# Down projection of f tiles 14 to 17 in seven products of quarters, with fewer weight buffers for it

## The chip, the cores and the metric

The kernel runs on one core of a Trainium2 chip. The time is device microseconds of one launch, the median of the runs. A profiled execution gives the trace. TensorE (PE) multiplies matrices, VectorE (DVE), ScalarE (ACT) and GpSimd (POOL) work on elements, SyncE (SP) issues DMAs; ScalarE and GpSimd can issue DMAs too.

## What is computed

A decoder trunk of two layers for 512 prompt tokens and 8 sequences of 8 sampled tokens, 576 columns together, with a model width of 1024, in float32. Layer 0 begins with a convolution and windowed attention (mixer 0), layer 1 with a Mamba-2 mixer (mixer 1); both then have the feed-forward part that the change is about:

```python
def conv_ffn(h, hist, w_gate, w_up, conv_w, conv_b, w_down):
    gate = h @ w_gate
    padded = jnp.concatenate([hist, gate], axis=1)
    gc = causal_dwconv(padded, conv_w, conv_b)
    y = (jax.nn.silu(gc) * (h @ w_up)) @ w_down
    return y, padded[:, -(FFN_CONV_WIDTH - 1):]
```

w_gate and w_up are 1024 x 2816, w_down is 2816 x 1024: 22 tiles (f = 0 to 21) of 128. Conv states, caches and SSM states are further outputs.

## The kernel before

Everything stays on the chip, transposed: x[m] (m = 0 to 7) are tiles of 128 channels x 576 columns. The columns are cut in two halves of 288. Every operand of a product is split into a high part that TensorE's fast float32 form holds, and the rest. A product of tiles is three matmuls (high by high, high by low, low by high), each 128x128 by 128x288, into one bank of PSUM. ScalarE makes the high part (a copy), VectorE the low part (a difference).

**Gate and up.** The class Strassen does two f tiles at a time in seven products of 12 matmuls where a plain form has eight (p1 to p7, in the Winograd form). It needs sums of weight quarters S1 to S4. `load` fetches the raw weights: the two upper quarters into a buffer `wr` of 1024 columns (`self.up`), the lower right quarter into another (`self.low`), and four slots st0 to st3 of 512 columns are first loaded with one quarter each by SyncE and then get others added by GpSimd's DMAs (`accum_op=ADD`). `alpha`, `beta` and `gamma` split the upper quarters, S1 with S2, and S4 with S3; `sums` splits the lower right one (`dh`, `dl`). The raw buffers come from one ring of three, tag `wr`; down weights use the same ring.

**Order.** In `ffn` the list todo holds 19 jobs after the first ones (Gate 4, Up 2, Gate 6, Up 4, ..., Up 20). In each turn the new job's first products alternate with the last products of the job before (`prev.p3`, `prev.p7`, `prev.p4`), and `some(1)` sets one tile of the down projection between them: 12 matmuls (four f tiles), for one output tile m and one half. `PARTS` cuts the down projection by f into (0, 2), (2, 6), (6, 10), (10, 14), (14, 18), (18, 22); here called parts 0 to 5. Part p starts when its last f tile is ready, part 5 is done after the loop by `out_proj`. `down` takes, per output tile, a buffer's half of down weights (`single` splits it to `vh`, `vl`), eight matrix products of quarters per pair of output tiles, one add to x[m] each (`add_x`). In layer 1 the last job's last product ends around 1440 us of the span; behind each layer's loop the rest of the down projection follows.

The order on each engine is fixed when the program is built, by a scheduler that works with costs of its own and with the pools' free buffers; so a change of buffers can move instructions elsewhere too. `keep_in_program_order` pins the first matmul of a product. `S` hands out slots of 576 columns, 48 small ones and EXTRA further.

## Time and profile before

| | us |
|---|---|
| median of 3 runs | 1482.55 (1481.72 to 1483.52) |
| profiled execution | 1483.3 |
| its span | 1481.5 |
| TensorE busy | 1459.2 (99%) |
| VectorE busy | 1119.0 (76%) |
| ScalarE busy | 822.0 (55%) |
| GpSimd busy | 304.1 (21%) |

The granted clock of TensorE is 0.995 over the span. Busy times come from the page. A matmul's length overlaps the next one's, so TensorE's busy time says only that something was always in flight. In the rows, L with a number is the line of the kernel, `<-` stands between outputs and inputs, and what stands in brackets is the idle time before the instruction with the engine and tile that ended it.

### The profile page before, as it was taken

To read this page: it belongs to the slowest core of one execution; us is meant where nothing else is said; L and a number is where in the kernel's file an instruction comes from. 1 tells how busy PE (TensorE), PEld (TensorE's weight loads), DVE (VectorE), ACT (ScalarE), POOL (GpSimd) and SP (SyncE) were. 2 spreads that over 40 slices of the span, in tenths; PEclk is the share of its full clock that TensorE was granted. 3 is DMA by queue.
4 is the path that set the end of the run, shared out by engine and by line. 5 is a ranking of instruction groups with operands and counts; after the bars stand their busy time and mean duration, and the time that the engine had idled before them with its cause. 6 is when DMAs were issued, how large, how long until landed. Compare 5 with 4: busy or idle time off the path is not lost.

```text
span 1481.5 us, 29273 instructions
## 1 busy us (share of the span) xinstructions
PE 1459.2 (99%) x11179; PEld 1389.9 (94%) x11179; DVE 1119.0 (76%) x2121; ACT 822.0 (55%) x1659; POOL 304.1 (21%) x517
## 2 busy tenths in 40 slices
PE   8999999999999999999999999999999999999999
PEld 7967799999999999998988998997999999999998
DVE  7968799876666665878897777776989766666673
ACT  6357467655445543487764665665457554444450
POOL 0026211222222220011203102102022222232300
PEclk9999999999999999999999999999999999999999
DMA  7604553787777772136245245245366787877841
GB/s 228 164 29 118 160 133 100 195 212 197 184 200 197 191 191 69 58 121 199 72 154 178 86 124 165 86 146 166 105 172 176 193 217 184 211 195 179 212 113 65
DMA packets 120779, 227.60 MB, mean 154 GB/s; under 512 B 25518, under 2 KB 32558, under 8 KB 120638
## 3 DMA queue, kind: packets, MB, share of 16 engines
q1 hardware_dynamic: 98750, 185.87, 39.7%
q0 software_dynamic: 21888, 39.86, 16.3%
q8 instruction: 88, 1.44, 0.4%
q14 instruction: 53, 0.43, 0.1%
HBM read 190.54 MB, written 15.21 MB: 139 GB/s over the span
## 4 chain that ended last, share of the span: by engine, by line
PE 86%; DVE 6%; ACT 4%; DMA 2%; issue 1%; SPq 0%; ACTq 0%; POOL 0%; DVEq 0%
PE mm L313 15%; PE mm L317 15%; PE mm L316 15%; PE x L113 5%; PE x L116 5%; PE x L117 5%; PE y L116 3%; PE y L117 3%; PE y L113 3%; PE mm L622 2%; PE mm L618 2%; PE mm L621 2%; PE z L116 1%; PE z L113 1%; PE z L117 1%; DMA acb<-acd 1%
## 5 line engine op out<-in xcount | busy, mean ns | idle before, releaser
L313 PE MATMUL mm<-hh,wh 128*128 128x288 f32 x864 | 261.0, 303 | 6.0 <-ACT wh L284 5.4
L316 PE MATMUL mm<-hl,wh 128*128 128x288 f32 x864 | 258.8, 300 | 0.9 <-DVE hl L801 0.8
L317 PE MATMUL mm<-hh,wl 128*128 128x288 f32 x864 | 257.5, 298 | 0.5 <-DVE wl L285 0.5
L497 DVE TENSOR_TENSOR x<-x,mm 128x288 f32<-128x288 f32 x288 | 128.6, 449 | 77.6 <-PE mm L317 76.3
L313 PEld LDWEIGHTS mm<-hh,wh 128*128 128x128 f32 x864 | 163.6, 190 | 14.3 <-ACT wh L284 5.9
L313 PE MATMUL mm<-yh,vh 128*128 128x288 f32 x576 | 170.0, 295 | 0.0
L316 PE MATMUL mm<-yl,vh 128*128 128x288 f32 x576 | 169.9, 295 | 0.0
L317 PE MATMUL mm<-yh,vl 128*128 128x288 f32 x576 | 169.8, 295 | 0.0
L316 PEld LDWEIGHTS mm<-hl,wh 128*128 128x128 f32 x864 | 163.5, 189 | 4.4 <-issue 1.6
L317 PEld LDWEIGHTS mm<-hh,wl 128*128 128x128 f32 x864 | 163.6, 189 | 3.5 <-issue 1.6
L284 ACT ACTIVATE wh<-wr 128x1024 fp32r<-128x1024 f32 (+1 forms) x97 | 101.6, 1048 | 102.6 <-PE mm L316 79.0
L285 DVE TENSOR_TENSOR wl<-wr,wh 128x1024 fp32r<-128x1024 f32 (+1 forms) x97 | 119.5, 1236 | 36.3 <-ACT wh L284 35.5
L82 ACT ACTIVATE wh<-st 128x512 fp32r<-128x512 f32 x152 | 91.3, 626 | 57.8 <-PE z L116 36.0
L69 POOL DMA_DIRECT2D st<-st x76 | 67.5, 889 | 262.8 <-DMA st<-st 65.5
L313 PE MATMUL mm<-yh,wh 128*128 128x288 f32 x384 | 115.9, 302 | 0.7 <-DVE x L497 0.7
L317 PE MATMUL mm<-yh,wl 128*128 128x288 f32 x384 | 115.0, 300 | 0.0
L316 PE MATMUL mm<-yl,wh 128*128 128x288 f32 x384 | 114.9, 300 | 0.0
L83 DVE TENSOR_TENSOR wl<-st,wh 128x512 fp32r<-128x512 f32 x152 | 101.3, 688 | 15.9 <-ACT wh L82 12.3
L316 PEld LDWEIGHTS mm<-yl,vh 128*128 128x128 f32 x576 | 108.4, 188 | 0.0
L317 PEld LDWEIGHTS mm<-yh,vl 128*128 128x128 f32 x576 | 108.3, 188 | 0.0
L313 PEld LDWEIGHTS mm<-yh,vh 128*128 128x128 f32 x576 | 108.3, 188 | 0.0
L573 DVE SCALAR_TENSOR_TENSOR gconv<-gbuf,par,gconv 128x592 f32<-128x592 f32 x88 | 73.0, 832 | 32.2 <-ACT gconv L571 31.6
(409 smaller groups left out, 4306.4 us busy)
## 6 DMA issues: line engine op xcount, KB each, us to landing
st<-in_w_up SPq DMA_DIRECT2D x80, 256.0 KB, 4.3
wr<-in_w_down SPq DMA_DIRECT2D x80, 256.0 KB, 3.5
wr<-in_w_in_o SPq DMA_DIRECT2D x40, 512.0 KB, 3.6
st<-st POOLq DMA_DIRECT2D x76, 256.0 KB, 4.7
st<-in_w_gate SPq DMA_DIRECT2D x72, 256.0 KB, 4.6
wr<-in_w_gate SPq DMA_DIRECT2D x26, 512.0 KB, 4.3
wr<-in_w_up SPq DMA_DIRECT2D x24, 512.0 KB, 4.1
st<-in_w_up POOLq DMA_DIRECT2D x40, 256.0 KB, 4.7
```

The lines of the kernel that those rows point to most:

```text
L82: nc.scalar.activation(hi, src, AF.Copy)
L83: nc.vector.tensor_tensor(lo, src, hi.bitcast(F32), op=SUB)
L113: m = nc.tensor.matmul(out, hi[:, ws], xh, start=first and k == 0, stop=False, skip_group_check=skip)
L116: nc.tensor.matmul(out, hi[:, ws], xl, start=False, stop=False, skip_group_check=skip)
L117: nc.tensor.matmul(out, lo[:, ws], xh, start=False, stop=k == 3, skip_group_check=skip)
L284: nc.scalar.activation(hi[:, a:b], raw[:, a:b], AF.Copy)
L285: nc.vector.tensor_tensor(lo[:, a:b], raw[:, a:b], hi[:, a:b].bitcast(F32), op=SUB)
L313: first = nc.tensor.matmul(out, hi[:, ws], xh[:, sl], start=i == 0, stop=False)
L316: nc.tensor.matmul(out, hi[:, ws], xl[:, sl], start=False, stop=False)
L317: nc.tensor.matmul(out, lo[:, ws], xh[:, sl], start=False, stop=i == n - 1)
L497: nc.vector.tensor_tensor(self.x[m][:, sl], self.x[m][:, sl], p[:, :HB], op=ADD)
L573: nc.vector.scalar_tensor_tensor(cv[:, :592], g[:, k:592 + k], w(k), cv[:, :592], op0=MUL, op1=ADD)
```

## The change

`SEVEN = (4,)` sends part 4 (f = 14 to 17) through `down7`: the f tiles are cut in a left pair (14, 15) and a right pair (16, 17), the output tiles in pairs m, m + 1, the columns in the two halves, and the same seven products of quarters are formed as for gate and up, six matmuls each: 42 in place of 48 per pair of output tiles. `quarters_of` forms the activation quarters (B11, B21, B22, T1 to T4) once per layer with `combine` and `operand`; the weight sums s1 to s4 are formed on VectorE for each pair of output tiles, and each of three buffers of 512 columns (`single`) and one `dd` is split. A product is added to, or subtracted from, x[m] right after its matmuls (`add`): seven adds per pair in place of four. Partial results of one pair stay in two banks, `dx` and `dy`, which later products add to.

To make room, S3 and S4 are no longer loaded: GpSimd's DMAs add the other quarters to the upper weights where they lie, after `alpha` has split these. So `self.up` is held until `gamma`. The lower right quarter goes to a slot of its own, `a22`. During the job loop two of the three buffers are for upper weights (`ring_up`) and one for down weights (`ring_wr`); behind the loop they are one ring again. The conv state that is read (`fhist`) and the one that is written share one slot, there is one more slot in all, and wide tiles take odd slots.

```diff
+SEVEN = (4,)
...
-        self.up = b.weights_load(up, 1024)
-        s1, s2, s3, s4 = self.s = [b.S(f"st{i}", 512) for i in range(4)]
-        for s, first, more in ((s1, low[:, 512:1024], low[:, 0:512]), (s2, up[:, 0:512], s1), (s4, up[:, 512:1024], s2),
-                               (s3, up[:, 0:512], low[:, 0:512])):
-            self.nc.sync.dma_start(s, first)
+        self.up = b.weights_load(up, 1024, b.ring_up)
+        s1, s2 = [b.S(f"st{i}", 512) for i in range(2)]
+        s3, s4 = self.up[:, 0:512], self.up[:, 512:1024]
+        self.s = s1, s2, s3, s4
+        self.nc.sync.dma_start(s1, low[:, 512:1024])
+        self.nc.sync.dma_start(s2, up[:, 0:512])
+        self.low = b.S("a22", 512)
+        self.nc.sync.dma_start(self.low, low[:, 512:1024])
+        self.alpha()
+        for s, more in ((s1, low[:, 0:512]), (s2, s1), (s3, low[:, 0:512]), (s4, s2)):
             self.nc.gpsimd.dma_start(s, more, accum_op=ADD)
-        self.low = b.weights_load(low[:, 512:1024], 512)
-        self.alpha()
...
-    EXTRA = 14
+    EXTRA = 15
...
+        self.ring_wr = [0, 1, 2]
...
-    def weights_load(self, src, n):
-        raw = self.wp.tile([P, 1024], F32, tag="wr", bufs=3, name="wr")
+    def weights_load(self, src, n, ring=None):
+        ring = ring or self.ring_wr
+        ring.append(ring.pop(0))
+        raw = self.wp.tile([P, 1024], F32, tag=f"wr{ring[-1]}", bufs=1, name="wr")
...
-        hist, so = self.S("fhist", NF * 16), self.S("fso", NF * 16)
+        hist = so = self.S("fhist", NF * 16)
...
+        def down7(p):
...
+            def quarters_of(name):
+                if name == "B22":
+                    t[name] = [operand("yq", v[:, right]) for v in vs]
+                elif name == "T1":
+                    t[name] = [operand("yT", combine(u[:, left], u[:, left], u[:, right], SUB)) for u in us]
...
+            def add(m, half, bank, op):
+                x = self.x[m][:, HALF[half]]
+                nc.vector.tensor_tensor(x, x, bank[:, :HB], op=op)
+
+            load(0)
+            first = self.single(raw[0][:, 0:2 * n])
+
+            def go():
+                for m in range(0, 8, 2):
+                    a11, a12, a21, a22 = [raw[m][:, i * n:i * n + n] for i in range(4)]
+                    w = self.single(raw[m][:, 0:2 * n]) if m else first
+                    s12, s43 = self.S("sd", 512), self.S("sd", 512)
+                    s1, s2, s4, s3 = s12[:, 0:n], s12[:, n:2 * n], s43[:, 0:n], s43[:, n:2 * n]
+                    nc.vector.tensor_tensor(s1, a21, a22, op=ADD)
+                    nc.vector.tensor_tensor(s2, s1, a11, op=ADD)
+                    x, z = self.ps("dx"), self.pm()
+                    product(x[:, :HB], w, 0, t["B11"], True)
+                    add(m, 0, x, ADD)
+                    product(z[:, :HB], w, n, t["B21"], True)
+                    add(m, 0, z, ADD)
+                    w = self.single(s12[:, 0:2 * n])
+                    nc.vector.tensor_tensor(s3, a11, a21, op=ADD)
+                    nc.vector.tensor_tensor(s4, a12, s2, op=ADD)
...
+                    nc.scalar.activation(dh, a22, AF.Copy)
+                    nc.vector.tensor_tensor(dl, a22, dh.bitcast(F32), op=SUB)
+                    load(m + 2)
...
+                    yield
+                    y = self.ps("dy")
+                    product(y[:, :HB], w, 0, t["T1"], True)
+                    add(m + 1, 1, y, SUB)
+                    product(x[:, :HB], w, n, t["T2"], False)
+                    add(m, 1, x, ADD)
+                    w = self.single(s43[:, 0:2 * n])
...
+                    yield
+                    product(y[:, :HB], w, 0, t["B22"], False)
+                    add(m, 1, y, ADD)
+                    product(x[:, :HB], w, n, t["T3"], False)
+                    add(m + 1, 1, x, SUB)
...
+                    yield
+                    product(x[:, :HB], (dh, dl), 0, t["T4"], False)
+                    add(m + 1, 0, x, SUB)
...
+        self.ring_up, self.ring_wr = self.ring_wr[:2], self.ring_wr[2:]
...
-                tiles = down(ready)
+                tiles = (down7 if ready in SEVEN else down)(ready)
...
+        self.ring_wr = self.ring_up + self.ring_wr
```

TensorE issues 48 matmuls fewer, VectorE 108 instructions more, ScalarE 39 more (36 splits and 3 table loads, the latter in mixer 1), SyncE 76 DMAs fewer; GpSimd has as many as before. Lines move: the old L497 (add to x) is L506, L1243 is L1376, L1016 is L1149; L800 is the add of `down7`, L811, L812, L819 and L820 form its weight sums, L825 and L303 are VectorE's halves of its splits, L597 and L595 those of the activation quarters.

Three places show the move. The first is VectorE near the end of mixer 0: `ca` is the convolution's output, `lsum` the sum over channels for the layer norm (whose mean TensorE forms, `pm`). Before:

```order
L1016 TENSOR_SCALAR ca_2043<-mm_1977,par_72 128x512
L1243 TENSOR_TENSOR lsum_2069<-lsum_2069,ca_2043 128x288
L1017 TENSOR_SCALAR ca_2043<-mm_1978,par_72 128x64
L1243 TENSOR_TENSOR lsum_2069<-lsum_2069,ca_2043 128x288
L1246 TENSOR_TENSOR ca_395<-ca_395,pm_2082 128x288
```

Now:

```order
L1149 TENSOR_SCALAR ca_2043<-mm_1977,par_72 128x512
L89 TENSOR_TENSOR dl_3177<-a22_3166,dh_3176 128x512
L1376 TENSOR_TENSOR lsum_2069<-lsum_2069,ca_2043 128x288
L1150 TENSOR_SCALAR ca_2043<-mm_1978,par_72 128x64
L1376 TENSOR_TENSOR lsum_2069<-lsum_2069,ca_2043 128x288
L1379 TENSOR_TENSOR ca_395<-ca_395,pm_2082 128x288
```

The low part of the first job's lower right weights (`a22`, in the old kernel a `wr` buffer, split much later) now stands between a step of `ca` and its sum.

The second is SyncE at the end of layer 1's loop. `st` and `a22` and the `wr` from `in_w_up` belong to jobs, the `wr` from `in_w_down` to the down projection. Before:

```order
L68 DMA st3_17614<-in_w_up 128x512
L68 DMA st2_17613<-in_w_up 128x512
L68 DMA st1_17612<-in_w_up 128x512
L273 DMA wr_17623<-in_w_up 128x512
L273 DMA wr_17717<-in_w_down 128x512 x2
L783 DMA out_ffn_p<-fpo_13433 128x44
L782 DMA out_ffn_s<-fso_13431 128x352
L273 DMA wr_17904<-in_w_down 128x512 x2
L273 DMA wr_18001<-in_w_down 128x512 x2
L273 DMA wr_18066<-in_w_down 128x512 x2
L273 DMA wr_18131<-in_w_down 128x512 x2
L273 DMA wr_18196<-in_w_down 128x512 x2
```

Now:

```order
L282 DMA wr_17568<-in_w_up 128x1024
L71 DMA st1_17571<-in_w_up 128x512
L73 DMA a22_17574<-in_w_up 128x512
L70 DMA st0_17570<-in_w_up 128x512
L916 DMA out_ffn_p<-fpo_13425 128x44
L915 DMA out_ffn_s<-fhist_13423 128x352
L282 DMA wr_17987<-in_w_down 128x512 x2
L282 DMA wr_17641<-in_w_down 128x512 x2
L282 DMA wr_18052<-in_w_down 128x512 x2
L282 DMA wr_17838<-in_w_down 128x512 x2
L282 DMA wr_18182<-in_w_down 128x512 x2
L282 DMA wr_18117<-in_w_down 128x512 x2
```

wr_17987, wr_18052, wr_18182 and wr_18117 are the final projection's chunks; the third and fourth pair's chunks of part 4 (wr_17641, wr_17838) stand among them, since they wait for the one buffer, and wr_18117 waits for wr_17838's.

The third is VectorE at the same place, where the last pairs of part 4 are added up. `mm`, `dx` and `dy` are PSUM banks, x0 to x7 the result, `gsilu` and `yl` activations. Before:

```order
L497 TENSOR_TENSOR x3_80<-x3_80,mm_17773 128x288
L294 TENSOR_TENSOR vl_17842<-wr_17717,vh_17841 128x512
L672 SCALAR_TENSOR_TENSOR gsilu_17162<-x_17418,gsilu_17162 128x288
L336 TENSOR_TENSOR yl_17801<-gsilu_17162,yh_17800 128x576
L285 TENSOR_TENSOR wl_18070<-wr_18066,wh_18069 128x1024
L659 TENSOR_TENSOR st_13894<-st_13894,y_17759 128x288
L661 TENSOR_TENSOR gsilu_17470<-gsilu_17470,st_13894 128x288
L497 TENSOR_TENSOR x4_81<-x4_81,mm_17845 128x288
L336 TENSOR_TENSOR yl_17838<-gsilu_17470,yh_17837 128x576
L657 SCALAR_TENSOR_TENSOR st_13894<-st_13894,x_17639 128x288
```

Now:

```order
L800 TENSOR_TENSOR x4_81<-x4_81,dx_17813 128x288
L303 TENSOR_TENSOR vl_17913<-wr_17838,vh_17912 128x512
L820 TENSOR_TENSOR sd_17917<-wr_17838,sd_17916 128x256
L696 SCALAR_TENSOR_TENSOR gsilu_17552<-x_17594,gsilu_17552 128x288
L800 TENSOR_TENSOR x4_81<-x4_81,dy_17855 128x288
L345 TENSOR_TENSOR yl_17888<-gsilu_17552,yh_17887 128x576
L800 TENSOR_TENSOR x5_82<-x5_82,dx_17813 128x288
L303 TENSOR_TENSOR vl_17937<-sd_17916,vh_17936 128x512
L800 TENSOR_TENSOR x5_82<-x5_82,dx_17813 128x288
L506 TENSOR_TENSOR x0_77<-x0_77,mm_17994 128x288
L294 TENSOR_TENSOR wl_18121<-wr_18117,wh_18120 128x1024
L800 TENSOR_TENSOR x6_83<-x6_83,dx_17920 128x288
```

Where an add to x stood between splits of whole operands, adds of one pair now alternate with splits (L303) and sums (L820) of quarters, and the split of the final projection's third chunk (L294) stands ahead of the fourth pair's first add.

More of the change, by code (lines that the diff above doesn't have):

```diff
@@ L77, in sums @@
         self.d = b.S("dh", 512, F32R), b.S("dl", 512, F32R)
-        self.split(self.low[:, 0:512], *self.d)
+        self.split(self.low, *self.d)
+        b.free(self.low)
     def split(self, src, hi, lo):
@@ L102, in gamma @@
         self.w3 = self.two(self.s[3], self.s[2])
-        self.b.free(self.s[3], self.s[2])
     def product(self, bank, w, col, q, first):
@@ L176, in S @@
     def S(self, name, n=T, dt=F32, rows=P):
-        i = self.idle.pop(0)
+        i = next((i for i in self.idle if n <= T or i % 2), self.idle[0])
+        self.idle.remove(i)
         pool = self.sp if i < self.NSLOT else self.ep
@@ L579, in gate_done, with operand @@
             self.free(g, cv)
-        def up_done(f):
+        def operand(name, src, sign=1.0):
+            q = self.S(name, T, F32R)
+            hi, lo = q[:, 0:HB], q[:, HB:T]
+            nc.scalar.activation(hi, src, AF.Copy, scale=sign)
+            if sign < 0:
+                nc.vector.scalar_tensor_tensor(lo, src, sign, hi.bitcast(F32), op0=MUL, op1=SUB)
+            else:
+                nc.vector.tensor_tensor(lo, src, hi.bitcast(F32), op=SUB)
+            return q
+        def up_done(f):
+            for p in SEVEN:
+                a, b = PARTS[p]
+                if a <= f < b:
+                    y_of[f] = operand("yq", sl_of[f][:, HALF[0]]) if f < (a + b) // 2 else None
+                    return
             y_of[f] = self.pair("y")
@@ L725, in down, with product @@
             return go()
+        def product(out, w, col, xs, first):
+            hi, lo = w
+            for k, q in enumerate(xs):
+                ws = slice(col + k * P, col + k * P + P)
+                m = nc.tensor.matmul(out, hi[:, ws], q[:, 0:HB], start=first and k == 0, stop=False, skip_group_check=not first)
+                if k == 0:
+                    self.tc.keep_in_program_order(m)
+                nc.tensor.matmul(out, hi[:, ws], q[:, HB:T], start=False, stop=False, skip_group_check=not first)
+                nc.tensor.matmul(out, lo[:, ws], q[:, 0:HB], start=False, stop=k == len(xs) - 1, skip_group_check=not first)
@@ L781, in ffn @@
         some(16)
+        self.ring_wr = self.ring_up + self.ring_wr
         nc.sync.dma_start(d["ffn_s"][l], so)
         nc.sync.dma_start(d["ffn_p"][l], po)
-        self.free(so, hist, self.sr, list(self.hq.values()))
+        self.free(hist, self.sr, list(self.hq.values()))
         if next_norm:
```

43 lines of the change are left out of this document (added).

## The prediction

> **What bounds the kernel now.** I read the page's busy times and the chain of waits first, then TensorE's timeline, then VectorE's timeline and the stretches around the change, last the waits and the landing times of DMAs.
>
> ```profile
> span 1481.5 us, 29273 instructions
> PE 1459.2 (99%) x11179; PEld 1389.9 (94%) x11179; DVE 1119.0 (76%) x2121; ACT 822.0 (55%) x1659; POOL 304.1 (21%) x517
> PE 86%; DVE 6%; ACT 4%; DMA 2%; issue 1%; SPq 0%; ACTq 0%; POOL 0%; DVEq 0%
> ```
>
> TensorE is busy 99% of the span and holds 86% of the chain that ended last: a matmul taken away is worth its issue time, if nobody else then makes TensorE wait. That time is not the length shown for one matmul. From the timeline of TensorE near the end:
>
> ```profile
> 1423.75 0.30 PE L113 MATMUL x<-hqT,wh 128*128 128x288 f32 x1
> ...
> 1431.57 0.30 PE L317 MATMUL mm<-yh,vl 128*128 128x288 f32 x1
> 1431.70 0.30 PE L113 MATMUL x<-hqT,dh 128*128 128x288 f32 x1
> ```
>
> Between the first and the last of these starts lie 60 matmuls: (1431.70 - 1423.75) / 60 = 0.1325 us each, though each is shown as 0.30 long, since they overlap.
>
> The stretches of the feed-forward part, where the change sits (two of the job loop, then the end of its last jobs in layer 1), and a stretch of the Mamba mixer:
>
> ```profile
> 300.00:400.00 100.00, 100.00 (x755) 100.00 (x754) 67.55 (x122) 51.29 (x91) 27.29 (x48) 1.00 0.81 202
> 1120.00:1220.00 100.00, 100.00 (x756) 100.00 (x755) 79.15 (x151) 59.22 (x111) 24.58 (x46) 1.00 0.81 202
> 1404.00:1444.00 40.00, 40.00 (x304) 40.00 (x303) 28.35 (x50) 19.35 (x32) 3.89 (x7) 1.00 0.48 121
> 632.00:656.00 24.00, 24.00 (x177) 23.09 (x177) 21.95 (x41) 23.22 (x44) 5.26 (x10) 1.00 0.34 112
> ```
>
> Columns: stretch and length, then busy time of TensorE, its weight loads, VectorE, ScalarE, GpSimd, then clock, DMA share and GB/s. In the job loop TensorE never idles, VectorE has 68 to 79% and ScalarE 51 to 59%; the clock is full. VectorE keeps 71% at the loop's end. In the mixer ScalarE is full (23.2 of 24).
>
> **1. The matmuls.** Per layer four pairs of output tiles take 42 matmuls in place of 48: 24 fewer, 48 in the kernel. 48 x 0.1325 = **-6.4 us**. The products are the same shape and run at the same full clock.
>
> **2. VectorE at the end of part 4.** VectorE's timeline gives the time from one instruction's start to the next where neither waits:
>
> ```profile
> 1408.68 0.69 DVE L294 TENSOR_TENSOR vl<-wr,vh 128x512 fp32r<-128x512 f32 x1
> 1409.28 0.83 DVE L573 SCALAR_TENSOR_TENSOR gconv<-gbuf,par,gconv 128x592 f32<-128x592 f32 x1
> 1410.03 0.38 DVE L641 SCALAR_TENSOR_TENSOR gbuf<-st,x 128x224 f32<-128x224 f32 x1
> 1410.33 0.21 DVE L642 SCALAR_TENSOR_TENSOR gbuf<-st,x 128x64 f32<-128x64 f32 x1
> 1410.46 1.22 DVE L83 TENSOR_TENSOR wl<-wr,wh 128x1024 fp32r<-128x1024 f32 x1
> 1411.59 0.45 DVE L497 TENSOR_TENSOR x<-x,mm 128x288 f32<-128x288 f32 x1
> 1411.96 0.45 DVE L659 TENSOR_TENSOR st<-st,z 128x288 f32<-128x288 f32 x1
> ...
> 1424.33 0.76 DVE L336 TENSOR_TENSOR yl<-gsilu,yh 128x576 fp32r<-128x576 f32 x1
> 1424.99 0.69 DVE L294 TENSOR_TENSOR vl<-wr,vh 128x512 fp32r<-128x512 f32 x1
> ...
> 1431.90 0.45 DVE L497 TENSOR_TENSOR x<-x,mm 128x288 f32<-128x288 f32 x1 [1.00 <-PE mm L317]
> ```
>
> So 512 columns cost 0.60 us, 592 0.75, 224 0.30, 64 0.13, 1024 1.13, 288 0.37, 576 0.66; 256 lies between 224 and 288: 0.33. The last row also shows the way from TensorE: the product's last matmul starts at 1431.57, its add at 1431.90, 0.33 later, and takes 0.45.
>
> In the new order of layer 1, from the first gate-and-up step that lets the quarters be formed to part 4's last add, stand 54 instructions of 288 columns, 19 of 512, 15 of 256, and four each of 1024, 592 and 576, two of 224 and two of 64: 20.0 + 11.4 + 5.0 + 4.5 + 3.0 + 2.6 + 0.9 = 47.4 us. TensorE issues 406 matmuls beside them: 53.8 us. That is 88% against 71% now. It fits, but an add now often stands behind splits and sums, and products of one pair share a bank: the next one on it waits for the add. Without anything between, a revisit costs 0.33 + 0.45 = 0.78 us, and each pair has four; the order puts 5 to 24 other matmuls between (0.66 us or more), so on time they cost near nothing.
>
> The tight place is weights. Down weights now go through one buffer, and after the loop the fourth pair's chunk and the final projection's third chunk come through it too. Landing times at the end of layer 1 (from 1422, then 1414 to 1422), and over the run:
>
> ```profile
> wr<-in_w_down SPq DMA_DIRECT2D x6, 256.0 KB, 2.8
> ...
> wr<-in_w_down SPq DMA_DIRECT2D x4, 256.0 KB, 4.1
> ...
> wr<-in_w_down SPq DMA_DIRECT2D x80, 256.0 KB, 3.5
> ```
>
> and ScalarE's split of 1024 columns at that place:
>
> ```profile
> 1428.59 1.06 ACT L284 ACTIVATE wh<-wr 128x1024 fp32r<-128x1024 f32 x1 [2.01 <-PE z L116]
> ```
>
> Count from the last matmul of the third pair's T2 product: add at 0.33, a 512 split at 0.70, the sum that reads the buffer last at 1.30 to 1.72, the load's two halves issued by 2.2 (0.43 apart, row below), landed at 5.0 with 2.8 us or 5.7 with 3.5, ScalarE's half done at 6.1 or 6.8, VectorE's at 7.2 or 7.9, and only then, behind it in VectorE's queue, the fourth pair's first add, done at 7.7 or 8.4. The T2 product that waits for it is 61 matmuls on, at 8.08. So the loss is 0 with 2.8, 0.3 with 3.5, 0.9 with 4.1. The chunk before it has the same shape. I take 0.5 for this place and 0.4 for the other adds that come late, 0.9 per layer, nearer to the quiet rows than to 4.1, since the loop's loads have ended by then: **+1.8**, between +0.2 (all at 2.8) and +6 (both chunks at 4.1, and adds behind them). [...]
>
> **3. The first job's low weights.** They have a buffer of their own now, so their load and split slip forward into mixer 0, where the VectorE order sets the split between two steps of the layer norm's sum.
>
> ```profile
> 172.75 0.75 DVE L1016 TENSOR_SCALAR ca<-mm,par 128x512 f32<-128x512 f32 x1 [2.92 <-PE mm L1006]
> 173.54 0.46 DVE L1243 TENSOR_TENSOR lsum<-lsum,ca 128x288 f32<-128x288 f32 x1
> ...
> 174.05 0.75 PE L1244 MATMUL pm<-lsum,o 128*128 128x288 f32 x2 [0.46 <-DVE lsum L1243]
> ...
> L68 SPq DMA_DIRECT2D st<-in_w_gate x4: 327/430/432, 169.1 to 170.4; - x4
> ...
> st<-in_w_gate SPq DMA_DIRECT2D x4, 256.0 KB, 3.6
> st<-in_w_up SPq DMA_DIRECT2D x4, 256.0 KB, 5.7
> ...
> 175.33 1.60 ACT L1248 ACTIVATE csq<-ca 128x288 f32<-128x288 f32 x4 [7.69 <-DVE ca L1246]
> ```
>
> SyncE issues four loads from 169.1, 0.43 apart; the third will be the low weights: 169.96 + 3.6 = 173.6. ScalarE is idle there and splits in about 0.6 (half of the 1024 row), VectorE follows at 174.2 for 0.60, and lsum starts at 174.8, not 173.5. TensorE already waits 0.46 for it, so 1.3 more, less the four matmuls (0.53) that now stand ahead: **+0.8**, between 0 (made up later) and +2.9 (landing at 5.7).
>
> **4. Mixer 1.** Other buffers give its instructions another order, and ScalarE loads its function tables 43 times in place of 40.
>
> ```profile
> 645.77 1.28 ACT L1295 ACT_TABLE_LOAD   x1
> 647.07 0.72 ACT L1295 ACTIVATE xs<-cconv,par 128x512 f32<-128x512 f32 x1
> ...
> PE pst L1613 <- ACT ysb L1604: 3.4, 2, 2.6
> ```
>
> Each costs 1.30 us to the next instruction on a full ScalarE. TensorE's waits there are few (the largest is the 3.4 shown): I take a third of 3 x 1.30 as felt, **+1.3**, between -1.5 (half of the wait shown goes) and +3.9. [...]
>
> **5. Costed at nothing.** The two sums no longer loaded but added up by GpSimd's DMAs where the upper weights lie; per job one buffer more to wait for, 76 loads fewer in all. Cover: GpSimd works 25 to 29% of the loop, and the sums are needed only a job later. What queues on SyncE:
>
> ```profile
> SPq L273 <- DVE vl L294: 25.3, 15, 4.1
> ACT dh L82 <- DMA wr<-in_w_gate: 13.9, 4, 6.0
> ```
>
> SyncE already stands up to 4.1 us for a down chunk's split, and the low weights come up to 6.0 us late for ScalarE, without a wait of TensorE in the loop. The shared conv state and the odd slots add nothing.
>
> **Sum.** -6.4 + 1.8 + 0.8 + 1.3 = -2.5 on the profiled execution's 1483.3 (1481.5 of span and 1.8 around it): 1480.8. The median of the runs, 1482.55, lies 0.75 lower: **1480.1 us**. A measurement of this kernel can tell 0.2%, 3.0 us, from no change, so this lies just inside.
>
> **Rivals.** *The whole gain*: chunks land at 2.8 and the new orders cost nothing: -6.4 + 0.4 gives 1476.5. For it speaks the full TensorE of every stretch above, against it the 88%. *VectorE becomes the bound at part 4's end*: an instruction that needs the one before it starts later,
>
> ```profile
> 1422.35 0.45 DVE L659 TENSOR_TENSOR st<-st,y 128x288 f32<-128x288 f32 x1 [1.14 <-PE y L117]
> 1422.84 0.46 DVE L661 TENSOR_TENSOR gsilu<-gsilu,st 128x288 f32<-128x288 f32 x1
> ```
>
> 0.49 and not 0.37. Were half of the 104 so, 6.2 us are added and VectorE has 53.6 of 53.8: I put 4 us per layer on TensorE, -6.4 + 8 + 2.1, some 1486.2. In the order only about ten pairs are so. *Slower*: SyncE. Forty down chunks of the loop now share one buffer; each load stands on SyncE until the chunk before is split, and the next job's weights queue behind it. The change loses from 0.16 us of TensorE per chunk (6.4/40); at 0.4 it is 16 - 6.4 + 3.9, about 1496. The 6.0 us of lateness that the loop takes today speaks against it.
>
> **Chances.** Forecast 0.52, with a range of its own from 1477.5 to 1483 (the drain at 0.3 to 1.9 per layer, mixers between their ends); whole gain 0.26; VectorE 0.14; SyncE 0.08. Of the forecast 0.21 lies below 1479.6 and 0.31 within 3.0 us. Faster 0.26 + 0.21 = 0.47; the same 0.31 and 0.09 of VectorE's milder cases, 0.40; slower 0.05 + 0.08 = 0.13. The range from 1475.6 to 1486 takes in the whole gain and most of VectorE's case.
>
> **What would show it.** Right: TensorE idle for 0.5 to 2 us between the last jobs and the final projection in each layer, released by adds of the new products; VectorE near 88% there; the wait for lsum in mixer 0 near 1.8 us; no TensorE wait in the job loop. Wrong: waits of TensorE inside the loop, or mixer 1 longer or shorter by over 3 us.

## The result and the profile after

| | before | after |
|---|---|---|
| median of 4 runs, us | 1482.13 (1479.58 to 1483.52) | 1499.25 (1494.9 to 1504.1) |
| ratio to before | | 1.0118, interval 1.0084 to 1.0153 |
| profiled execution, its span | 1483.3, 1481.5 | 1500.31, 1498.5 |

The change makes the kernel 1.2% slower, some 17 us. The forecast was 1480.1, with 1486.0 as the upper end.

The page after, the lines that answer to the first ones of the prediction (span, busy times, chain of waits, landing times; SPq and POOLq are the queues of SyncE and GpSimd, in which their DMAs are issued):

```profile
span 1498.5 us, 29217 instructions
PE 1460.0 (97%) x11131; PEld 1383.0 (92%) x11131; DVE 1150.3 (77%) x2229; ACT 829.3 (55%) x1698; POOL 305.8 (20%) x517
PE 71%; DVE 12%; DMA 9%; ACT 4%; issue 3%; SPq 0%; POOL 0%; ACTq 0%; DVEq 0%; POOLq 0%
wr<-in_w_down SPq DMA_DIRECT2D x80, 256.0 KB, 5.8
wr<-st POOLq DMA_DIRECT2D x38, 256.0 KB, 7.2
```

TensorE has 48 matmuls fewer and yet its share of the chain falls from 86 to 71%: VectorE has 12% of it and DMAs 9%, where they had 6 and 2. A down chunk now lands in 5.8 us and not in 3.5. The sums that GpSimd's DMAs add up in place (`wr<-st`) land in 7.2.

Where the time went is read from two views. First the stretches of the job loop of layer 0 (240 to 530), its end (530 to 600), the handoff to mixer 1 (600 to 640) and the loop of layer 1 (1140 to 1380); before:

```profile
240.00:530.00 290.00, 290.00 (x2185) 290.00 (x2184) 209.49 (x383) 159.86 (x296) 79.22 (x135) 1.00 0.76 192
530.00:600.00 70.00, 70.00 (x529) 70.00 (x529) 43.70 (x82) 28.41 (x50) 7.46 (x18) 1.00 0.42 115
600.00:640.00 40.00, 39.14 (x313) 36.23 (x312) 32.12 (x69) 23.00 (x51) 4.62 (x13) 1.00 0.20 67
1140.00:1380.00 240.00, 240.00 (x1812) 240.00 (x1811) 165.86 (x305) 123.52 (x224) 66.25 (x110) 1.00 0.79 196
```

and after:

```profile
240.00:530.00 290.00, 287.23 (x2157) 286.18 (x2157) 203.01 (x382) 152.21 (x291) 79.89 (x137) 1.00 0.68 161
530.00:600.00 70.00, 64.78 (x472) 62.70 (x471) 57.75 (x125) 33.50 (x63) 7.68 (x17) 1.00 0.41 111
600.00:640.00 40.00, 37.79 (x285) 34.00 (x284) 29.53 (x68) 16.94 (x40) 1.32 (x10) 0.96 0.16 53
1140.00:1380.00 240.00, 236.66 (x1775) 235.72 (x1774) 164.44 (x304) 120.88 (x225) 67.45 (x115) 1.00 0.70 168
```

The first count in brackets is the matmuls that TensorE had in flight in the stretch, two or three of them begun just before it. It is a better ruler here than the busy time: 28 fewer in the loop of layer 0 are 28 x 0.1325 = 3.7 us lost, though only 2.8 us look idle, since a matmul is shown 0.30 long and so covers the first part of each wait. By this ruler the end of layer 0's loop loses 57 x 0.1325 = 7.6 us, the stretch of layer 1's loop 4.9.

Second, the time between the same matmuls in both traces (from the timelines of TensorE). A loop is counted from the first product of its first job to the first product into `z` of its 17th, its end from there to the last job's last product; "rest" is the final projection and whatever follows it, the 12 removed matmuls of each "end" and "rest" included. The first f tiles ahead of each loop (39.2 and 39.1 us before, 39.2 and 39.4 after) are left out:

| stage | before | after | difference |
|---|---|---|---|
| mixer 0, up to the feed-forward part | 214.0 | 212.7 | -1.3 |
| job loop, layer 0 | 266.2 | 269.9 | +3.7 |
| end of that loop | 50.9 | 56.2 | +5.3 |
| rest of the down projection, norm, mixer 1 | 511.6 | 515.9 | +4.3 |
| job loop, layer 1 | 265.7 | 270.6 | +4.9 |
| end of that loop, then rest | 85.7 | 85.7 | 0.0 |

They add up to 16.9 of the 17.0 us. Both job loops, the end of the first and mixer 1 lose, and the sum includes the 6.4 us that were to be won.

**The loop.** What TensorE waits for in 240 to 530 after (us in total, times, longest; before, this view has no line):

```profile
PE x L118 <- DVE gbuf L666: 1.2, 1, 1.2
PE mm L322 <- DVE x L506: 0.9, 1, 0.9
PE z L118 <- DVE x L506: 0.6, 1, 0.6
```

In the loop of layer 1 it waits 2.0 us for `z` and 1.1 us for `gbuf`. The first wait above, followed back through the timelines of SyncE, ScalarE, VectorE and TensorE:

```profile
291.08 0.85 SPq L282 DMA_DIRECT2D wr<-in_w_down  x2
293.83 0.33 SPq L73 DMA_DIRECT2D a<-in_w_up  x1
...
301.19 0.63 ACT L88 ACTIVATE dh<-a 128x512 fp32r<-128x512 f32 x1 [6.60 <-DMA wr<-st]
301.73 0.77 ACT L580 ACTIVATE gconv<-gbuf,par 128x592 f32<-128x592 f32 x1
302.54 0.84 DVE L582 SCALAR_TENSOR_TENSOR gconv<-gbuf,par,gconv 128x592 f32<-128x592 f32 x1 [4.72 <-ACT gconv L580]
304.67 0.22 DVE L666 SCALAR_TENSOR_TENSOR gbuf<-st,x 128x64 f32<-128x64 f32 x1
304.94 0.40 PE L118 MATMUL x<-hqT,dh 128*128 128x288 f32 x1 [1.25 <-DVE gbuf L666]
```

The low weights (`a`, short for a22) are issued at 293.83, behind the two loads of a down chunk, and land 4.9 us later, at 298.8. ScalarE reaches their split `dh` at 294.6 and stands there for 6.6 us: 4.2 for the low weights and 2.4 more for the releaser named, a sum added in place (`wr<-st`), issued at 294.06 and landed 7.1 us later. The split does not read that sum; that `dh` was given a slot which the sum's DMA still reads would fit, but the trace does not name slots. In ScalarE's queue behind `dh` stands the convolution of the gate, behind that VectorE's, and TensorE waits 1.25 us for the bank that VectorE was to empty.

The longest wait of layer 1's loop comes from the low weights alone:

```profile
1204.82 1.55 SPq L73 DMA_DIRECT2D a<-in_w_gate  x1
...
1214.43 0.63 ACT L88 ACTIVATE dh<-a 128x512 fp32r<-128x512 f32 x1 [6.68 <-DMA a<-in_w_gate]
1215.09 0.69 DVE L89 TENSOR_TENSOR dl<-a,dh 128x512 fp32r<-128x512 f32 x1 [6.62 <-ACT dh L88]
1215.70 0.45 DVE L506 TENSOR_TENSOR x<-x,mm 128x288 f32<-128x288 f32 x1
1216.20 0.40 PE L118 MATMUL z<-hqB,wh 128*128 128x288 f32 x1 [2.04 <-DVE x L506]
```

They took 9.6 us to land. ScalarE's half of their split waits for them, VectorE's half (`dl`) for that, the add to x behind it in VectorE's queue is late, and TensorE waits 2.04 us for the bank that the add was to empty. The waits of ScalarE at these splits in 240 to 530 (us in total, times, longest):

```profile
ACT dh L82 <- DMA wr<-in_w_gate: 13.4, 7, 5.7
ACT dh L82 <- DMA wr<-in_w_up: 5.4, 4, 2.4
```

That was before; after:

```profile
ACT dh L88 <- DMA a<-in_w_gate: 30.6, 6, 7.3
ACT dh L88 <- DMA a<-in_w_up: 13.4, 4, 7.1
ACT dh L88 <- DMA wr<-st: 6.6, 1, 6.6
```

From 18.8 us in 11 waits to 50.6 in 11, and the longest from 5.7 to 7.3.

**The end of the first loop.** ScalarE's, VectorE's and TensorE's timelines after:

```profile
560.84 0.42 ACT L824 ACTIVATE dd<-wr 128x256 fp32r<-128x256 f32 x1 [3.42 <-DMA wr<-in_w_down]
561.29 0.43 DVE L825 TENSOR_TENSOR dd<-wr,dd 128x256 fp32r<-128x256 f32 x1 [3.35 <-ACT dd L824]
563.74 0.45 DVE L800 TENSOR_TENSOR x<-x,dy 128x288 f32<-128x288 f32 x1
564.34 0.37 PE L755 MATMUL dy<-yq,vh 128*128 128x288 f32 x1 [2.26 <-DVE x L800]
```

A down chunk of the next pair comes late through the one buffer; its two loads, the last issued at 554.00, took 6.5 and 6.8 us to land. Its last quarter's split (`dd`) stands in the queues of ScalarE and VectorE ahead of the work of the pair that TensorE is at. VectorE stands 3.35 us for it, and the add that TensorE needs (L800) comes behind it.

### The profile page after: what moved, and what is told of

Same layout as the page of the kernel before. It is cut to its first block, busy times and chain, and to the rows that moved or that the text cites. A ratio compares the mean times of both kernels' runs of the same rounds, so it can differ in the third digit from the quotient of the medians.

```text
span 1498.5 us, 29217 instructions
## 1 busy us (share of the span) xinstructions
PE 1460.0 (97%) x11131; PEld 1383.0 (92%) x11131; DVE 1150.3 (77%) x2229; ACT 829.3 (55%) x1698; POOL 305.8 (20%) x517
## 4 chain that ended last, share of the span: by engine, by line
PE 71%; DVE 12%; DMA 9%; ACT 4%; issue 3%; SPq 0%; POOL 0%; ACTq 0%; DVEq 0%; POOLq 0%
PE mm L326 13%; PE mm L322 13%; PE mm L325 13%; PE x L118 4%; PE x L121 4%; PE x L122 4%; DMA wr<-in_w_down 3%; PE y L122 2%; PE y L121 2%; PE y L118 2%; PE mm L646 2%; PE mm L642 2%; PE mm L645 2%; DMA st<-in_w_gate 1%; DVE wl L294 1%
## 5 line engine op out<-in xcount | busy, mean ns | idle before, releaser
L506 DVE TENSOR_TENSOR x<-x,mm 128x288 f32<-128x288 f32 x256 | 113.4, 447 | 44.6 <-PE mm L326 43.7
L294 DVE TENSOR_TENSOR wl<-wr,wh 128x1024 fp32r<-128x1024 f32 (+1 forms) x97 | 121.7, 1258 | 29.6 <-ACT wh L293 29.0
L322 PE MATMUL mm<-yh,vh 128*128 128x288 f32 x448 | 132.3, 295 | 0.9 <-DVE x L506 0.9
L326 PE MATMUL mm<-yh,vl 128*128 128x288 f32 x448 | 132.4, 296 | 0.0
L325 PE MATMUL mm<-yl,vh 128*128 128x288 f32 x448 | 132.3, 295 | 0.0
L88 ACT ACTIVATE wh<-wr 128x512 fp32r<-128x512 f32 (+1 forms) x114 | 82.8, 763 | 30.6 <-PE z L121 20.3
L89 DVE TENSOR_TENSOR wl<-wr,wh 128x512 fp32r<-128x512 f32 (+1 forms) x114 | 96.6, 861 | 2.9 <-ACT wh L88 2.4
L118 PE MATMUL x<-hqT,wh 128*128 128x288 f32 x304 | 89.8, 295 | 0.9 <-ACT st L125 0.9
L121 PE MATMUL x<-hqT,wh 128*128 128x288 f32 x304 | 89.7, 295 | 0.0
L122 PE MATMUL x<-hqT,wl 128*128 128x288 f32 x304 | 89.5, 294 | 0.0
L322 PEld LDWEIGHTS mm<-yh,vh 128*128 128x128 f32 x448 | 84.3, 188 | 1.2 <-DVE x L506 1.2
```

The lines of the kernel that those rows point to most:

```text
L88: nc.scalar.activation(hi, src, AF.Copy)
L89: nc.vector.tensor_tensor(lo, src, hi.bitcast(F32), op=SUB)
L118: m = nc.tensor.matmul(out, hi[:, ws], xh, start=first and k == 0, stop=False, skip_group_check=skip)
L121: nc.tensor.matmul(out, hi[:, ws], xl, start=False, stop=False, skip_group_check=skip)
L122: nc.tensor.matmul(out, lo[:, ws], xh, start=False, stop=k == 3, skip_group_check=skip)
L294: nc.vector.tensor_tensor(lo[:, a:b], raw[:, a:b], hi[:, a:b].bitcast(F32), op=SUB)
```

## The experiments

Two kernels serve as bases. *Slots only* is the kernel before with the small parts of the change: one slot for the conv states, one more slot, odd slots for wide tiles. *Seven only* adds `down7` to it. The other kernels put single parts of the change into them or take parts out of the changed kernel. Each batch had its own runs of before: medians from 1481.26 to 1482.44.

**1. The changed kernel without the seven products.**

```diff
-SEVEN = (4,)
+SEVEN = ()
```

> The changed kernel with part 4 again in eight products (down projection as before), all buffer changes kept. Theory A (the buffers cost the time: one buffer for down weights and two held for upper weights, with the low weights behind them on SyncE): the job loops still lose 8 to 9 us and mixer 1 some 5, nothing is gained, 1482 + 13 = about 1495, and TensorE still waits near the start of each loop. Theory B (the seven products cost it, by late splits on VectorE and ScalarE): the loops and the ends are clean, 1482 to 1487.

Measured: 1494.19 (1491.42 to 1494.81), ratio 1.0078 [1.0063, 1.0093]. So most of the loss does not come from the seven products: the room that was made for them costs 12 us alone.

**2. The seven products alone**: loads, sums and the shared ring of three as before.

> The seven products with the weights loaded as before (S3 and S4 in slots of their own, low weights in the ring, one ring of three buffers shared with the down weights); the conv states share a slot and there is one slot more. Theory A: loops clean, ends lose 1 to 4 us in all, mixer order unlike both: 1476 to 1482. Theory B: the ends still lose 10 us or more, 1486 to 1490.

Measured: 1480.0 (1477.36 to 1483.11, 10 runs), ratio 0.9987 [0.9977, 0.9996]. It is 19 us faster than the changed kernel, and the one that beats both kernels, though by less than 0.2% against before. Its loops, in the stretches of above:

```profile
240.00:530.00 290.00, 289.97 (x2183) 289.41 (x2183) 212.27 (x397) 157.06 (x297) 74.49 (x132) 1.00 0.78 195
1140.00:1380.00 240.00, 240.00 (x1810) 240.00 (x1809) 166.81 (x305) 123.01 (x224) 61.73 (x115) 1.00 0.81 203
```

2183 and 1810 matmuls, against 2185 and 1812 before: nothing is lost there.

**3. Slots only.**

> The kernel before with only the conv states in one slot, one slot more and wide tiles in odd slots: e2 without the seven products. It gives the price of the other order in mixer 1 alone. If that order costs 2 us: 1484 to 1485, and the seven products themselves are worth 4 to 5 us against it. If it costs nothing: 1482, and the seven products keep only 2 of their 6.4 us.

Measured: 1480.51 (1477.66 to 1485.39, 12 runs), ratio 0.9991 [0.9978, 1.0004]: no cost, as the prediction had it. Against it the seven products gain 0.5 us by the medians, which the spread of the runs covers, not 6.4 and not the 4.6 that were left after the adds. The profiled execution of slots only, 1484.88, lies near the top of its range and loses 6 us in the loop of layer 0 (272.5 against 266.5 with seven only): there too `dh` waits, 7.05 us for weights in the ring, and TensorE 3.0 us behind it. By the other stages of the two traces, the end of loop 0 is 1.1 us shorter than with slots only (49.7 to 50.8), mixer 1 with the rest of the down projection ahead of it 2.1 longer (511.4 to 509.3), the end of loop 1 1.0 shorter (49.7 to 50.7) and the last stretch 0.8 (34.2 to 35.0): 0.8 in all. So 2.9 of the 4.8 us due in three of these stages come, 1.9 are lost to adds and splits, and 3.7 are lost where mixer 1 begins or in it; why, no run tells.

**4. The ring of three split into two and one, low weights in a slot, S3 and S4 loaded into slots.**

> Eight products; the buffers split two and one and the low weights in a slot as in the change, but S3 and S4 loaded into slots of their own as before, so that the upper weights' buffer is free after its split. Mixers in the same order as in e1. If the single down buffer is what costs (theory A1): as e1, within 2 us. If it is the sums added up in place, which hold the upper buffers and bunch the DMAs (theory A2): the loops lose nothing and it is 7 to 9 us faster than e1, about 1487.

Measured: 1502.06 (1495.01 to 1504.99), ratio 1.0128 [1.01, 1.0155]. The loss is there in full without the sums in place, which neither theory has: 7.9 us more than in experiment 1, from which this kernel differs by the sums alone. With the slot and the split ring there, adding S3 and S4 up in place makes the kernel faster. Of the 7.9 us, 4.7 stand ahead of the loop of layer 1 (44.0 against 39.3 us).

**5. The changed kernel with one shared ring of three.**

```diff
-        ring = ring or self.ring_wr
-        ring.append(ring.pop(0))
-        raw = self.wp.tile([P, 1024], F32, tag=f"wr{ring[-1]}", bufs=1, name="wr")
+        raw = self.wp.tile([P, 1024], F32, tag="wr", bufs=3, name="wr")
...
-        self.ring_up, self.ring_wr = self.ring_wr[:2], self.ring_wr[2:]
+        self.ring_up = None
...
-        self.ring_wr = self.ring_up + self.ring_wr
```

As in the kernel before, the pool now hands out the three buffers, and not a list that the kernel keeps.

> The changed kernel, sums in place and seven products, but one ring of three buffers shared by upper and down weights all through. A1: the loops' waits go, about as e2, 1478 to 1484. A2: the loops still lose 8 us or more, 1488 to 1496.

Measured: 1487.58 (1484.46 to 1489.88), ratio 1.0036 [1.0023, 1.0049]. Some 12 us come back, in the end of loop 0 (51.9 instead of 56.2) and mixer 1 (511.7), 3.1 in the loop of layer 1, none in that of layer 0. That lies between the ranges of the two theories: the split, with the list that hands it out, costs the changed kernel 11.7 us, and the slot with the sums in place, by which this kernel differs from seven only, 7.6.

**6. The same with the low weights issued by GpSimd**, to take them out of SyncE's queue.

```diff
-        self.nc.sync.dma_start(self.low, low[:, 512:1024])
+        self.nc.gpsimd.dma_start(self.low, low[:, 512:1024])
```

> e4 (seven products, sums in place, one shared ring of three) with one change: the low weights are loaded from GpSimd's queue, ahead of its adding DMAs, and not from SyncE's behind the load of the upper weights, which now waits for a buffer held until gamma. Theory A2a (SyncE stands for that buffer, the low weights behind it come late, and ScalarE, which takes its work in order, stands at their split with the conv behind it): the waits of the job's last product (x<-hqT,dh, 2.3 and 1.2 us in e4) go, 3 to 5 us faster than e4, 1482 to 1485. Theory A2b (the sums in place bunch the DMAs, whatever queue): the waits stay, 1486 to 1489.

Measured: 1544.15 (1539.73 to 1547.04), ratio 1.0411 [1.0387, 1.0435]. Waits in the loop (ScalarE, GpSimd, TensorE):

```profile
ACT dh L88 <- DMA a<-in_w_gate: 47.9, 6, 10.1
...
POOL st L76 <- DMA st<-in_w_gate: 38.7, 9, 9.0
POOL a L73 <- DVE wl L89: 11.9, 5, 6.6
...
PE x L118 <- ACT st L125: 10.0, 3, 4.9
```

GpSimd's queue stands too, for the loads that it is to add to, and the low weights now stand behind that: `dh` waits up to 10.1 us and TensorE up to 4.9. The kernel loses 57 us by this one change of place, so GpSimd's queue, with its waits for data, is the worse place for this load. Whether TensorE feels the low weights or the sums behind them, which come later too, this run does not tell.

**7. and 8. Four buffers (two for upper weights, two for down), two slots less**, in the changed kernel and in that of experiment 1.

```diff
-    EXTRA = 15
+    EXTRA = 13
...
-        self.ring_wr = [0, 1, 2]
+        self.ring_wr = [0, 1, 2, 3]
```

> The changed kernel with a fourth weight buffer (two for upper, two for down weights) and two slots fewer. If the one down buffer causes the waits of z and mm after part 0, of the quarter products at the end of the loop and of mixer 1's start: loops lose only 1 to 2 us each (the low weights), the ends 1 each, mixer 1 1 to 2: 1482 to 1486. If it is the sums in place alone: 1494 to 1498.

> e1 (eight products, sums in place, ring split) with the same fourth buffer for down weights. One-buffer theory: the two loops take 268 us and less where e1 has 270.3 and 268.8, and mixer 1 goes back by 3 us or more: 1486 to 1489. Otherwise as e1, 1493 to 1496.

Measured: 1495.58 (1492.71 to 1501.08), ratio 1.0086 [1.0056, 1.0115], and 1495.44 (1492.19 to 1497.0), ratio 1.0082 [1.0062, 1.0103]. A second down buffer takes away the loss at the end of loop 0 (50.7 against 56.2): there the one buffer was the cause. The loops stay slow (276.4 and 273.3 in layer 0, where the kernels with three buffers take 269.9 and 270.3), so there it was not, and two slots less may add to it.

**9. Slots only, with the low weights in a slot.**

```diff
-        self.low = b.weights_load(low[:, 512:1024], 512)
+        self.low = b.S("a22", 512)
+        self.nc.sync.dma_start(self.low, low[:, 512:1024])
```

> e0 (eight products, old ring of three, sums in slots) with one step of the change: the lower right weights of a job go to a slot and not into the ring. Every kernel with slow loops so far has this step. Theory C1 (the slot: its load comes late, and ScalarE stands at its split): the loops lose 3 us or more each against e0, 1486 to 1492. Theories C2, C3: no loss, 1479 to 1483.

Measured: 1496.71 (1494.04 to 1501.52), ratio 1.0112 [1.0075, 1.015]: 16 us from where one tile lies. The loops take 270.9 and 272.3 (before 266.2 and 265.7), and the loop of layer 1 starts 5 us late: ScalarE waits 5.69 us for the first job's low weights, VectorE's work for the norm stands behind their split, and TensorE waits 3.4 us for it. In the changed kernel that start is 0.3 us late, so the 16 us are not the slot's price there.

**10. Slots only, with S3 and S4 added up in place.**

> e0 with one other step: S3 and S4 added up in the upper weights' buffer, which is held until gamma; the low weights stay in the ring of three, which now has to serve all. C2 (the buffer held stops SyncE and what is queued behind it): the loops lose 3 us or more each, 1487 to 1500. C1 alone: 1478 to 1483, with 38 loads fewer per layer.

Measured: 1502.33 (1499.81 to 1503.63), ratio 1.0145 [1.0121, 1.017]. The loops take 281.6 and 276.2; in layer 0's stretch:

```profile
240.00:530.00 290.00, 280.29 (x2069) 278.10 (x2069) 195.16 (x362) 146.20 (x277) 73.65 (x134) 0.98 0.68 160
```

and among SyncE's waits there:

```profile
SPq L278 <- DVE wl L87: 83.3, 13, 9.3
```

116 matmuls fewer than before, 15.4 us. SyncE stands 83 us for splits (`wl`), 23 with slots only: the buffer of upper weights is held until `gamma`, in a ring of three that serves the low weights too. In the changed kernel the low weights are not in that ring.

**11. Slots only, with the ring split into two and one, low weights among the upper ones.**

> e0 with the third step: two buffers for upper and lower right weights of jobs, one for down weights; sums in slots, as before. C3 (the one down buffer): the loops lose 3 us or more each and mixer 1 about 4, as in e1 and e3: 1489 to 1496. C1 or C2 alone: loops as e0; mixer 1 still tells whether its loss comes with the split.

Measured: 1483.89 (1482.85 to 1487.25), ratio 1.0018 [1.0008, 1.0029]:

```profile
240.00:530.00 290.00, 290.00 (x2190) 290.00 (x2188) 211.42 (x384) 158.85 (x292) 73.68 (x136) 1.00 0.78 196
600.00:640.00 40.00, 36.21 (x270) 32.14 (x269) 32.09 (x71) 24.12 (x52) 3.83 (x12) 0.96 0.17 54
```

One down buffer costs the loop nothing by itself. What this kernel loses stands in the handoff to mixer 1, 43 matmuls or 5.7 us; mixer 1 with what stands ahead of it takes 515.6 us, against 509.3 with slots only and 511.6 before.

**12. Seven only, with the weight sums on GpSimd instead of VectorE.**

```diff
-                    nc.vector.tensor_tensor(s1, a21, a22, op=ADD)
-                    nc.vector.tensor_tensor(s2, s1, a11, op=ADD)
+                    nc.gpsimd.tensor_tensor(s1, a21, a22, op=ADD)
+                    nc.gpsimd.tensor_tensor(s2, s1, a11, op=ADD)
```

(s3 and s4 likewise.)

> e2 (seven products alone) with the four weight sums of a pair formed by GpSimd and not by VectorE: 16 instructions per layer leave VectorE where it is fullest. If VectorE's queue at the end of the loop is what keeps the seven products from their 6.4 us: 1 to 2 us faster than e2, 1478 to 1479. If GpSimd stands at its DMAs and the sums come late: 1481 to 1486.

Measured: 1493.34 (1492.05 to 1496.89), ratio 1.0089 [1.0057, 1.0121]. Over the run TensorE now waits here:

```profile
PE dy L750 <- ACT vh L297: 9.7, 2, 7.3
```

The splits of the sums wait for GpSimd, whose sums stand behind waits of its own (`sd` up to 5.7 us for `wl` and 5.3 for `x` in 530 to 580). The ends of the loops grow from 49.7 to 56.6 and 60.6. VectorE at 90% is still the better place.

**13. The slot, with the ring's order restored.** What in experiment 9 costs: the slot itself, or that upper and down loads then share the ring in another order?

```diff
+        b.ring_wr.append(b.ring_wr.pop(0))
         self.low = b.S("a22", 512)
...
-        raw = self.wp.tile([P, 1024], F32, tag="wr", bufs=3, name="wr")
+        ring = ring or self.ring_wr
+        ring.append(ring.pop(0))
+        raw = self.wp.tile([P, 1024], F32, tag=f"wr{ring[-1]}", bufs=1, name="wr")
```

So that the ring can be turned, the kernel's own list hands out the buffers here.

> The kernel with low weights in a slot (1496.7), but at each job the ring of three is turned one place further, so that upper weights and down chunks share buffers as they did when the low weights stood in the ring; the low weights are still in slot a22. Theory A: the slot cost 15 us because, with the low weights out of the ring, upper weights and down chunks share buffers in turn, and an upper load stands on SyncE until the upper weights before are split (waits for wl of up to 12.9 us); then this one is back at 1480 to 1485. Theory B: the recycled slot comes free late, and what stands behind its load on SyncE is late; then this one stays at 1493 to 1500, with low weights late for dh by 4 us and more as before. Theory C: any place outside the ring changes the order on SyncE's queue enough; 1488 to 1500.

Measured: 1500.48 (1498.1 to 1502.61), ratio 1.0125 [1.0104, 1.0146]. Theory A falls: the loops are as slow as in experiment 9 (272.0 and 269.6), and ScalarE waits 58.9 us for the low weights in that of layer 0, where it waited 55.6. The order of the ring is not it. Mixer 1 is longer (518.7 against 510.9).

**14. A buffer of its own for the low weights, one slot less.**

```diff
-    EXTRA = 15
+    EXTRA = 14
...
-        self.low = b.S("a22", 512)
+        self.low = b.wp.tile([P, 512], F32, tag="a22", bufs=1, name="a22")
```

> The kernel with low weights in a slot, but the low weights have one buffer of 512 columns that nothing else uses (and one slot less, 14 extra); the ring of three holds upper weights and down chunks alone, as in the kernel with the slot. Theory A (ring shared in turn by upper and down): stays at 1490 to 1500, with SyncE's upper and down loads waiting for wl of upper weights. Theory B (recycled slot late): back at 1480 to 1485, since the low load now waits only for the split of the job before, which is done when the next job begins. Theory C (order of the queue): 1488 to 1500, with low weights late for dh.

Measured: 1484.02 (1480.52 to 1487.2, 10 runs), ratio 1.0015 [1.0002, 1.0029]. Of the 16 us all but 3.5 are gone. The load of a job's low weights (SyncE) and their split (ScalarE), with the slot of experiment 9:

```profile
279.44 0.33 SPq L73 DMA_DIRECT2D a<-in_w_up  x1
...
286.05 0.63 ACT L86 ACTIVATE dh<-a 128x512 fp32r<-128x512 f32 x1 [5.46 <-DMA a<-in_w_up]
```

and with a buffer of their own:

```profile
265.38 0.33 SPq L73 DMA_DIRECT2D a<-in_w_up  x1
...
279.44 0.62 ACT L85 ACTIVATE dh<-a 128x512 fp32r<-128x512 f32 x1
```

This load is issued 14 us earlier, and ScalarE finds its data. Over the jobs of layer 0 the median time from such a load to its split is 10.9 us, with the slot 5.9. The sums of ScalarE's waits over 240 to 530 say the same, first with the slot:

```profile
ACT dh L86 <- DMA a<-in_w_up: 40.6, 8, 6.7
ACT dh L86 <- DMA a<-in_w_gate: 15.0, 4, 4.5
```

and with the buffer, where this is the only wait of `dh` for a DMA:

```profile
ACT dh L85 <- DMA a<-in_w_gate: 2.3, 1, 2.3
```

Theory B forecast the time: a slot that goes round among many tiles takes the load of the low weights too late. How it does so is in part open. At the load itself SyncE stands no longer with the slot (24.8 us in 235 to 545, with the buffer 33.1); the load comes later in SyncE's queue, in the rows above behind two loads more into `st`, the upper weights and a down chunk. That the order was built so because the slot comes free late fits, but is not shown.

## Why the prediction was wrong

**Term 5, costed at nothing, is the step that failed first.** It said of sums in place, of a buffer more to wait for and of the slots: "GpSimd works 25 to 29% of the loop, and the sums are needed only a job later." Term 3 took the place of the low weights for "a buffer of their own"; it is a slot that goes round, and experiments 9 and 14 show that just this makes 12.7 us. Alone the slot costs 16 us (experiment 9 against 3) and the sums in place 22 (10 against 3), but these prices do not add up: with a shared ring the two cost 7.6 us together (experiment 5 against 2), and with the slot and the split ring there the sums in place gain 7.9 (1 against 4). In the changed kernel the two loops, where the prediction had no wait, lose 8.6 of the 17 us, by the late splits of the low weights shown above. No run gives the changed kernel a buffer of their own for them, so how much of the 8.6 would come back is open.

The cover was misread twice. GpSimd's busy share, 79.2 us of 290 before and 79.9 after, did not show what stood in its queue or in SyncE's: in experiment 14 the load was hidden by being issued 14 us earlier. And the 6.0 us that `dh` came late before, without a wait of TensorE, were read as cover, though waits little longer can be felt: 6.60 and 6.68 us in the changed kernel and 7.05 in the profile of slots only were, 7.32 at another place of the changed kernel was not.

**The other part is the ring split into two and one, priced too low in terms 2 and 4.** With the list that hands the buffers out it costs the changed kernel 11.7 us (experiment 5), at the end of layer 0's loop, in mixer 1 and in the loop of layer 1.

**The signs.** Both that were named for being wrong came: TensorE waits in both job loops, and mixer 1, with the rest of the down projection ahead of it, is 4.3 us longer.

**The rival "Slower: SyncE"** had the right chain for the loops (a load stands late on SyncE, the next job's weights behind it), with 0.08. Its place was wrong: alone, the one buffer for down chunks costs the loops nothing (experiment 11), and in the changed kernel sharing it gave 3.1 us back in the loop of layer 1 and none in that of layer 0. Its price of 16 us in the loops is twice the 8.6 that they lost, so that its sum, about 1496, came near to 1499 is partly luck.

**Term 1, the matmuls**: 48 fewer, as counted, at 0.1325. Right.

**Term 2, VectorE at the end of part 4, +1.8.** With seven only three of the four stages concerned lose 1.9 together (experiment 3), and VectorE is at 36 of 40 us there, 90% where 88 were forecast:

```profile
1406.00:1446.00 40.00, 39.83 (x298) 39.41 (x297) 35.94 (x74) 19.51 (x35) 4.25 (x7) 1.00 0.41 111
```

That size was right for three shared buffers. The mechanism, a late chunk in one buffer and the queue behind it (VectorE 3.35 us for `dd`, the add behind that, 2.26 us of TensorE), was right too, but was priced for one place of layer 1. In layer 0, where a late chunk took 6.5 and 6.8 us to land and is split by `dd` ahead of the pair at work, it cost 5.3 us and the 1.6 that 12 matmuls fewer should have won, 6.9, beyond the term's 6 for the whole kernel.

**Term 3, the first job's low weights, +0.8.** The wait forecast was 1.8 us; measured, over the run:

```profile
PE pm L1377 <- DVE lsum L1376: 1.9, 1, 1.9
```

Right, and by the mechanism forecast: `dl` at 171.41 stands ahead of `lsum` at 172.01. It does not come with the slot alone (0.5 in experiment 9), but where the sums are in place as well (2.0 in experiment 1, 1.5 in 5). Mixer 0 as a whole is shorter than before; the granted clock was 0.50 there for 10.2 us in the profile of before (12.2 to 15.6 and 145.3 to 152.1) and for 3.4 in that of after (from 173.5).

**Term 4, mixer 1, +1.3.** Measured with the rest of the down projection: 4.3 us longer though 12 matmuls fewer, 5.9 in all, and not by the table loads: slots only has 44 of them, four more than before, and a mixer 1 of 509.3, shorter than before. The loss sits in the handoff, where TensorE waits for `hh`, `wl` and `hl` of mixer 1's first products. It is there in experiments 1, 4, 11 and 13 and in the changed kernel, where three buffers are handed out by a list, and in none where the pool turns them by itself or there are four. In each of the five the granted clock over 600 to 640 is below full (0.91 in experiment 13, 0.96 in the rest; in the changed kernel it is 0.50 for 3.4 us from 630.9), in the others it is 1.00. Which wait begins it no run isolates.

**The rival "VectorE becomes the bound"** did not come: with VectorE at 36 of 40 us, seven only loses 1.9 us in three of the four stages, where that rival put 4 per layer; the 2.26 us that TensorE waited at the end of layer 0's loop came from a chunk that was 3.42 late. **"The whole gain"** is excluded by seven only.

## What to carry to other kernels

Price every load by where it will stand in its queue and when its place comes free, not by an engine's busy share: a tile that is moved into a place that others use too (12.7 us here, experiment 9 against 14), or one that is held a stage longer (22 us, experiment 10), must be costed as a late load, with all that stands behind the waiting instruction on its engine, as the add behind `dl` did that TensorE waited 2.04 us for. Where the trace shows such a wait without harm (6.0 us before), a little more of it may already be felt (6.60 after). Try the dearest "free" part alone first, and then in the kernel that it is meant for, since parts that cost 16 and 22 us alone cost 7.6 together. Count matmuls per stretch: they overlap here (shown 0.30 us long, begun 0.1325 apart), and in the loop of layer 0 only 2.8 us looked idle where 3.7 were lost.

## What was not expected of the hardware

A stall cost more than its own length here. In experiment 5 TensorE waits 2.08 us for `gbuf` at 304.96; the windows around it:

```profile
304.00:306.00 2.00, 1.04 (x8) 1.05 (x9) 2.00 (x5) 1.49 (x4) 0.38 (x2) 1.00 0.12 37
306.00:309.00 3.00, 3.00 (x16) 3.00 (x15) 3.00 (x8) 2.31 (x5) 2.19 (x5) 0.52 0.64 174
```

After the wait the granted clock is 0.52 in the second window, and 13 matmuls begin in it, 0.240 us apart, where 22 or 23 would: TensorE is busy throughout and yet loses time. By the timeline and the clock (0.91 from 309 to 312) the slow stretch is 3.4 us long and holds 15 matmuls, 3.5 us where 15 x 0.1325 = 2.0 would do, so it costs some 1.5. The length of a wait alone does not tell whether it comes: the 2.04 us in layer 1's loop of the changed kernel were not followed by it (clock 1.00 from 1216 to 1228), while in its handoff to mixer 1 a wait of 1.08 us and one of 0.34 us right behind it were (0.50 from 630.9 to 634.3). Sums in place have a clock of 0.98 over 240 to 530 and of 0.99 over 1140 to 1380, and seven only has 1.000 over the span. What decides whether a wait is followed by a slow stretch no run shows.
